# An encoder layer on one Trainium2 core: the 1024-token feed-forward block in two passes, its up-projection in seven block products

## The chip, the core and the metric

The kernel runs on one core of a Trainium2 chip. A core has five engines that run their own instruction queues in order and wait for one another by semaphores: PE (TensorE, matrix products), ACT (ScalarE), DVE (VectorE), POOL (GpSimd) and SP (SyncE, which issues nearly all of this kernel's DMAs). The metric is device time in microseconds (us) of one execution; lower is better.

## What is computed

One layer of an encoder with shared weights, on a request of 1024 tokens (the prompt) and one of 512 (the sample), width 1024, inner width 2816, all in float32:

```python
def encoder_layer(x, g_attn, w_in, ..., w_o, g_ffn, w_up, conv_w, conv_b, w_down):
    ...                                   # norm, attention in two branches, sigmoid gates: "merge"
    x = x + (g_a * a + g_b * bo) @ w_o
    u = dwconv(rmsnorm(x, g_ffn) @ w_up, conv_w, conv_b)      # w_up 1024 x 5632, conv of width 3 along the tokens
    u_gate, u_val = jnp.split(u, 2, axis=-1)
    return x + (jax.nn.gelu(u_gate) * u_val) @ w_down         # w_down 2816 x 1024

y = rmsnorm(encoder_layer(x, ...), g_final)
```

Only the last two lines of the layer and the final norm, and these for the prompt alone, are touched by the change: the feed-forward block, FFN from here on.

## The kernel before

Every float32 product is made of three matmuls on split operands: an operand is rounded to a `hi` part by ACT, and the rest, `lo = x - hi`, is made by DVE or POOL; then hi·hi, hi·lo and lo·hi are summed in PSUM (helper `mm3`, L147 to L149; for the down-projection L801 to L803 in `accumulate`). A matmul takes a 128x128 stationary block and streams 512 columns.

The sample runs first, then the prompt's attention, then `merge`, which leaves x as eight tiles `xacc` of 128 tokens x 1024, and then `ffn`. The order of each engine's instructions is fixed when the program is built; an engine never overtakes in its own queue.

`ffn` for the prompt (T = 1024, NT = 8 token tiles, FT = 22 channel blocks of 128):
- Norm, in two chunks of four token tiles: ACT sums the squares (L175) and takes the root (L176), DVE makes the reciprocal root in six small steps (L177 to L183) and `xn` (L190); PE transposes xn, eight times four 128x128 blocks a chunk (L198), ACT makes `hhi` from PSUM (L202) and DVE `hlo` (L203).
- For each of the 22 channel blocks: `wload` of 128 columns of w_up for the gate and for the value (a 512 KB DMA into `raw`, ACT makes `whi`, L138, DVE every third time and POOL otherwise make `wlo`, L141). `conv` sums 8 blocks of K over both halves of 512 tokens (L147 to L149), and ACT and DVE make the convolution (L831, L832, L834), GELU (L843) and the product (L848); ACT and POOL split it into `ghi`, `glo` (L851, L852).
- After every second channel block, `accumulate` multiplies the two blocks by their rows of w_down (L801 to L803) and DVE adds the sums to `xacc` (L805), so x stays in SBUF for the whole block and is updated eleven times.
- At the end the final norm, tile by tile (yo, L869), and a DMA for each tile.

The weights of the first channel blocks are loaded and split while `merge` still runs, since `raw`, `whi` and `wlo` come from pools that `merge` and `ffn` share.

Of the kernel before, what the change touches and what calls it, by code (L numbers as in the profile page):

```python
# [118 lines left out]
class _Layer:  # L119
# [687 lines left out]
    def ffn(self, ctx, hooks, xnp):  # L807
# [57 lines left out]
        for tt in range(NT):  # L865
# [3 lines left out]
            nc.vector.scalar_tensor_tensor(out=y, in0=x, scalar=rs, in1=gf, op0=ALU.mult, op1=ALU.mult)  # L869
            nc.sync.dma_start(self.y_dram[tt * P:(tt + 1) * P, :], y)  # L870

    def begin(self, ctx, x_dram, y_dram, T, side):
        self.x_dram, self.y_dram, self.side = x_dram, y_dram, side
        self.T, self.NT, self.NH, self.KPU = T, T // P, T // 512, 1024 // T
        self.stat_d = self.dram.tile([3, T, 8], F32, tag=f"stat{T}", name=f"stat{T}")
        self.frow_d = self.dram.tile([20, T], F32, tag=f"frow{T}", name=f"frow{T}")
        self.o_d = self.dram.tile([3, 2, P, T], F32, tag=f"o{T}", name=f"o{T}")
        self.ab_d = self.dram.tile([4, P, T], F32, tag=f"ab{T}", name=f"ab{T}")
        self.v_d = self.dram.tile([2, T, 512], F32, tag=f"v{T}", name=f"v{T}")
        self.hp = self.pool(ctx, "hp", 2 * KT // self.KPU)  # L880
# [17 lines left out]
def hybrid_encoder_kernel(ctx: ExitStack, tc: tile.TileContext, x_prompt, x_sample, g_attn, w_in, b_gate, rel_bias, sink,  # L898
# [63 lines left out]
    class _Taps:  # L962
        starts = (120, 164, 76)

        def __getitem__(self, key):
# [3 lines left out]

    w = {"w_in": w_in[0], "w_a_out": w_a_out[0], "w_b_out": w_b_out[0], "w_o": w_o[0], "w_up": w_up[0],  # L970
         "w_down": w_down[0]}
    raws = ctx.enter_context(tc.tile_pool(name="raw", bufs=3))
    split = ctx.enter_context(tc.tile_pool(name="split", bufs=3))

    class _W:
        def tile(self, *a, tag, **kw):
# [5 lines left out]
    with ExitStack() as s_ctx, ExitStack() as p_ctx:  # L982
        sample.begin(s_ctx, x_sample[0], y_sample[0], 512, left)
        with ExitStack() as a_ctx:
            sample.begin_norm(a_ctx, right)
            rp = a_ctx.enter_context(tc.tile_pool(name="rows", bufs=1, side=right, reuse_waits="tile"))
            sample.attention(a_ctx, bias_rows(rp))
        with ExitStack() as n_ctx:
            def begin_prompt():
                prompt.begin(p_ctx, x_prompt[0], y_prompt[0], 1024, right)  # L990
                prompt.begin_norm(n_ctx, right)
                return prompt.xin, "xin"
            sample.finish({11: lambda *a: prompt.norm_in(0, 4, *a), 15: lambda *a: prompt.norm_in(4, 4, *a)}, begin_prompt)
        s_ctx.close()
        with ExitStack() as a_ctx:
            prompt.attention(a_ctx, None)
        prompt.finish({})


# [24 lines left out]
```

## Time and profile before

| | us |
|---|---|
| median of three runs | 2368.64 (2364.14 to 2368.64) |
| the profiled execution | 2362.39, of it span 2360.6 |
| busy in the span: PE, DVE, ACT, POOL | 2273.1 (96%), 1110.5, 881.5, 563.6 |
| FFN of the prompt, first transposition to last matmul | 1592.2 to 2346.6 |
| from the last matmul to the end of the span | 14.0 |

All times below are from the start of the span. "Busy" of PE counts a matmul from its issue to its modelled end, and matmuls overlap: the mean duration of a matmul (395 ns) is not what it costs; the distance from one start to the next is. A group of rows shows what ended the idle time before its instructions, behind the arrow.

### The profile page before, as it was taken

To read this page: it belongs to the slowest core of one execution; us is meant where nothing else is said; L and a number is where in the kernel's file an instruction comes from. 1 tells how busy PE (TensorE), PEld (TensorE's weight loads), DVE (VectorE), ACT (ScalarE), POOL (GpSimd) and SP (SyncE) were. 2 spreads that over 40 slices of the span, in tenths; PEclk is the share of its full clock that TensorE was granted. 3 is DMA by queue.
4 is the path that set the end of the run, shared out by engine and by line. 5 is a ranking of instruction groups with operands and counts; after the bars stand their busy time and mean duration, and the time that the engine had idled before them with its cause. 6 is when DMAs were issued, how large, how long until landed. Compare 5 with 4: busy or idle time off the path is not lost.

```text
span 2360.6 us, 27878 instructions
## 1 busy us (share of the span) xinstructions
PE 2273.1 (96%) x10890; PEld 1864.3 (79%) x10890; DVE 1110.5 (47%) x1957; ACT 881.5 (37%) x1554; POOL 563.6 (24%) x296
## 2 busy tenths in 40 slices
PE   7999899899999999999999999999999999999997
PEld 6887687688878788898777788877888888888885
DVE  4547523644554535645784434335333433343336
ACT  5657422533443345655673111134212222212223
POOL 2121354333333210011002332231222212212220
PEclk9999999999999999999999999999999999999999
DMA  5553543333333312332118311112111111111101
GB/s 160 150 173 93 159 137 91 110 97 97 116 106 91 113 49 68 116 111 72 44 45 224 109 44 50 41 54 63 45 45 45 42 48 54 45 54 45 45 27 71
DMA packets 232856, 197.76 MB, mean 84 GB/s; under 512 B 18129, under 2 KB 203169, under 8 KB 232725
## 3 DMA queue, kind: packets, MB, share of 16 engines
q1 hardware_dynamic: 232440, 195.89, 27.6%
q8 instruction: 85, 1.39, 0.3%
q14 instruction: 47, 0.38, 0.1%
q10 hardware_dynamic: 284, 0.11, 0.0%
HBM read 175.19 MB, written 27.06 MB: 86 GB/s over the span
## 4 chain that ended last, share of the span: by engine, by line
PE 75%; DVE 3%; ACT 2%; issue 1%; POOL 0%; DMA 0%; POOLq 0%; ACTq 0%; DVEq 0%; SPq 0%
PE psu L147 10%; PE psu L149 10%; PE psu L148 10%; PE pacc L803 6%; PE pacc L802 6%; PE pacc L801 6%; PE psg L148 3%; PE psg L149 3%; PE psg L147 3%; PE pso L409 2%; PE pst L395 1%; PE psq L149 1%; PE psq L147 1%; PE psq L148 1%; PE psk L147 1%; PE psk L148 1%
## 5 line engine op out<-in xcount | busy, mean ns | idle before, releaser
L141 POOL TENSOR_TENSOR wlo<-raw,whi 128x1024 fp32r<-128x1024 f32 (+1 forms) x164 | 387.3, 2368 | 1170.3 <-ACT whi L138 946.3
L138 ACT CAST whi<-raw 128x1024 fp32r<-128x1024 f32 (+1 forms) x244 | 250.4, 1035 | 768.9 <-PE pacc L803 293.6
L805 DVE TENSOR_TENSOR xacc<-xacc,pacc 128x512 f32<-128x512 f32 x420 | 285.3, 686 | 303.2 <-PE pacc L803 301.0
L147 PE MATMUL psu<-hhi,whi 128*128 128x512 f32 x1056 | 416.5, 395 | 0.2 <-ACT hhi L202 0.2
L149 PE MATMUL psu<-hhi,wlo 128*128 128x512 f32 x1056 | 416.5, 395 | 0.0
L148 PE MATMUL psu<-hlo,whi 128*128 128x512 f32 x1056 | 416.3, 395 | 0.0
L141 DVE TENSOR_TENSOR wlo<-raw,whi 128x1024 fp32r<-128x1024 f32 (+1 forms) x80 | 103.8, 1298 | 328.2 <-ACT whi L138 305.6
L147 PEld LDWEIGHTS psu<-hhi,whi 128*128 128x128 f32 x1056 | 198.4, 188 | 46.5 <-ACT hhi L202 1.3
L149 PEld LDWEIGHTS psu<-hhi,wlo 128*128 128x128 f32 x1056 | 198.7, 188 | 45.8
L148 PEld LDWEIGHTS psu<-hlo,whi 128*128 128x128 f32 x1056 | 198.7, 188 | 45.6
L801 PE MATMUL pacc<-whi,ghi 128*128 128x512 f32 x528 | 209.5, 397 | 5.8 <-ACT ghi L851 4.2
L803 PE MATMUL pacc<-whi,glo 128*128 128x512 f32 x528 | 209.9, 398 | 2.3 <-POOL glo L852 2.3
L802 PE MATMUL pacc<-wlo,ghi 128*128 128x512 f32 x528 | 208.9, 396 | 0.0
L852 POOL TENSOR_TENSOR glo<-y,ghi 128x512 fp32r<-128x512 f32 (+1 forms) x44 | 81.1, 1842 | 451.4 <-ACT ghi L851 451.4
L832 DVE SCALAR_TENSOR_TENSOR y<-psu,vecs,y 128x511 f32<-128x511 f32 (+1 forms) x88 | 89.1, 1012 | 138.6 <-ACT y L831 138.6
L147 PE MATMUL psg<-hhi,whi 128*128 128x512 f32 x384 | 151.8, 395 | 1.2 <-ACT frow L505 1.2
L149 PE MATMUL psg<-hhi,wlo 128*128 128x512 f32 x384 | 151.7, 395 | 0.0
L148 PE MATMUL psg<-hlo,whi 128*128 128x512 f32 x384 | 151.6, 395 | 0.0
L801 PEld LDWEIGHTS pacc<-whi,ghi 128*128 128x128 f32 x528 | 99.6, 189 | 30.9 <-ACT ghi L851 5.1
L803 PEld LDWEIGHTS pacc<-whi,glo 128*128 128x128 f32 x528 | 99.5, 189 | 29.2 <-POOL glo L852 5.8
L802 PEld LDWEIGHTS pacc<-wlo,ghi 128*128 128x128 f32 x528 | 99.7, 189 | 23.4
L783 DVE TENSOR_TENSOR sg<-sg,psa 128x512 f32<-128x512 f32 x48 | 32.9, 687 | 157.1 <-PE psa L149 122.9
(150 smaller groups left out, 4156.1 us busy)
## 6 DMA issues: line engine op xcount, KB each, us to landing
raw<-in_w_up_dram SPq DMA_DIRECT2D x88, 512.0 KB
raw<-in_w_in_dram SPq DMA_DIRECT2D x80, 512.0 KB
raw<-in_w_down_dram SPq DMA_DIRECT2D x44, 512.0 KB
raw<-in_w_o_dram SPq DMA_DIRECT2D x16, 512.0 KB
skew<-rows SPq DMA_DIRECT2D x24, 256.0 KB
v<-vs SPq DMA_DIRECT2D x24, 256.0 KB
v<-v SPq DMA_DIRECT2D x24, 256.0 KB
out_dram<-yo SPq DMA_DIRECT2D x12, 512.0 KB
```

Of the source, the lines that this page charges most:

```text
L138: nc.scalar.copy(out=hi[:, :n], in_=raw[:, :n])
L141: eng.tensor_tensor(out=lo[:, :n], in0=raw[:, :n], in1=hi[:, :n].bitcast(F32), op=ALU.subtract)
L147: mm(out, whi, r[0], start=start, stop=False)
L148: mm(out, whi, r[1], start=False, stop=False)
L149: mm(out, wlo, r[0], start=False, stop=stop)
L409: mm(o[:, o0 * P:(o0 + n) * P], v[kt], p[:, c0 * P:(c0 + n) * P], start=i == 0, stop=i == total - 1)
L801: mm(p, a, whi[:, cols], start=i == 0, stop=False)
L802: mm(p, a, wlo[:, cols], start=False, stop=False)
L803: mm(p, b, whi[:, cols], start=False, stop=i == len(parts) - 1)
L805: nc.vector.tensor_tensor(out=x, in0=x, in1=p, op=ALU.add)
L832: nc.vector.scalar_tensor_tensor(out=y[:, 1:T], in0=ps[:, 0:T - 1], scalar=tap[0], in1=y[:, 1:T], op0=ALU.mult, op1=ALU.add)
L852: nc.gpsimd.tensor_tensor(out=lo, in0=yv, in1=hi.bitcast(F32), op=ALU.subtract)
```

## The change

The prompt's FFN is taken apart into three stages (`finish_strassen`); the sample's is as before.

`quads`: the same norm, but each chunk of four token tiles (a half of 512 tokens) is scaled by g and kept as float32 (`ht`, L905), x itself goes out to DRAM (`xres`, L897), and out of the four quadrants (two halves of K = 1024 by two halves of tokens) b11, b21, b12, b22 four combinations are made: t1 = b12 - b11, t3 = b22 - b12, t2 = b22 - t1, t4 = b21 - t2 (L915, three quarters on DVE and one quarter on POOL). The seven right operands b11, b21, t1, t2, t3, t4 and b22 are each split into hi and lo (L885, L886).

`up_strassen`: gate and value columns of a channel block are the two block rows of the left operand, and the two halves of K its block columns, so that a 2 x 2 by 2 x 2 block product gives gate and value for both halves of tokens. It is done by seven products of 12 matmuls (4 blocks of K, three each) in place of eight. POOL makes the four sums of weights (`rsum`, L968); `ring_split` makes hi (ACT, L938) and lo (DVE, L939) of each of the seven left operands in a ring of seven buffers, five products ahead. The products are summed in three PSUM banks A, B, C; ACT copies a bank out (L979, L983, L985, L988: `ug`, `uv`) and DVE adds B or C (L976). Convolution, GELU and product are as before, from SBUF in place of PSUM, and the result `gv` goes out to DRAM (L1004).

`down`: for each half of 512 tokens eight PSUM banks (4 token tiles by 2 halves of the width) sum over all 22 blocks (24 matmuls a step, L1056 to L1058); each step loads its 512 columns of `gv` (`graw`, L1036) and the 128 rows of w_down (`wraw`, L1038) into a ring of four buffers and splits them, three ring_splits a step. After the 22nd step DVE adds the eight sums to x, read back from DRAM (L1050), and the final norm of four tiles follows.

```diff
+    def quads(self, hc, psum, sm):
...
+        def split(name, src, pool, tag):
+            hi, lo = ([pool.tile([P, 2, H], F32R, tag=tag, name=f"{name}{s}") for _ in range(2)] for s in ("hi", "lo"))
+            for j in range(4):
+                h, l = hi[j // 2][:, j % 2], lo[j // 2][:, j % 2]
+                nc.scalar.copy(out=h, in_=src(j))
+                nc.vector.tensor_tensor(out=l, in0=src(j), in1=h.bitcast(F32), op=ALU.subtract)
...
+        for half in range(2):
...
+            for tt, (x, xn, rs) in enumerate(zip(xs, xns, self.rstd(xs, sm, lambda: next(left)))):
+                nc.vector.tensor_scalar(out=xn, in0=x, scalar1=rs, scalar2=None, op0=ALU.mult)
+                nc.sync.dma_start(self.x_d[half * 4 + tt], x)
...
+                    nc.tensor.transpose(ps[:, i * P:(i + 1) * P], xn[:, k * P:(k + 1) * P], self.c["ident"])
...
+                nc.scalar.activation(out=tiles[-1][:, k % 2], in_=ps, func=AF.Identity, scale=g[:, k:k + 1])
+                if half == 0 and k % 4 == 3:
+                    t = tiles[-2:]
+                    split(f"b{k // 4 + 1}1", lambda j: t[j // 2][:, j % 2], self.hp, "h")
...
+                eng = nc.gpsimd if j == 3 else nc.vector
+                eng.tensor_tensor(out=out[j], in0=in0[j], in1=in1[j], op=ALU.subtract)
+            split(name, lambda j: out[j], pool, tag)
+        combine("t1", b12, b11, b11, self.hp, "h")
+        t1 = b11
+        combine("t3", b22, b12, b12, hc, "hc")
+        split("b22", lambda j: b22[j], hc, "hc")
+        combine("t2", b22, t1, b22, self.hp, "h")
+        combine("t4", b21, b22, b21, hc, "hc")
...
+    def product(self, out, w, quad, start):
...
+        for j in range(4):
+            cols = slice(j * P, (j + 1) * P)
+            hi, lo = self.q[quad][j]
+            for n, (a, b) in enumerate(((whi, hi), (whi, lo), (wlo, hi))):
+                mm(out, a[:, cols], b, start=start and j == 0 and n == 0, stop=j == 3 and n == 2, skip_group_check=True)
...
+    def ring_split(self, src):
...
+        nc.scalar.copy(out=hi, in_=src)
+        nc.vector.tensor_tensor(out=lo, in0=src, in1=hi.bitcast(F32), op=ALU.subtract)
...
+    def up_strassen(self, ctx, psum):
...
+        for i in range(FT + 1):
+            cur = ["m1", "m2", "m5", "m6"] if i < FT else []
+            old = ["m4", "m3"] if i else []
+            order += [(i, m) for m in cur] + [(i - 1, m) for m in old] + ([(i, "m7")] if i < FT else [])
...
+                for out, a, b, op in ((s[0], blk("v", 0), blk("v", 1), ALU.add), (s[1], s[0], blk("g", 0), ALU.subtract),
+                                      (s[2], blk("g", 0), blk("v", 0), ALU.subtract), (s[3], blk("g", 1), s[1], ALU.subtract)):
+                    nc.gpsimd.tensor_tensor(out=out, in0=a, in1=b, op=op)
...
+            if m == "m1":
+                g["ug"], g["uv"] = (up.tile([P, T], F32, tag="uy", name=n) for n in ("ug", "uv"))
+                nc.scalar.copy(out=g["ug"][:, left], in_=g["A"])
...
+        where = {"m1": ("A", "b11"), "m2": ("B", "b21"), "m5": ("C", "t1"), "m6": ("A", "t2"), "m7": ("A", "t3"),
+                 "m4": ("A", "t4"), "m3": ("C", "b22")}
...
+    def down(self, ctx, psum):
...
+        def prepare(half, k):
+            graw = self.rraw.tile([P, 512], F32, tag="rraw", name="graw")
+            nc.sync.dma_start(graw, self.gv_d[k][:, half * 512:half * 512 + 512])
+            wraw = self.rraw.tile([P, D], F32, tag="rraw", name="wraw")
+            nc.sync.dma_start(wraw, W["w_down"][k * P:(k + 1) * P, :])
+            return self.ring_split(graw), [self.ring_split(wraw[:, nh * 512:nh * 512 + 512]) for nh in range(2)]
...
+                    mm(p, a, whi, start=k == 0, stop=False)
+                    mm(p, a, wlo, start=False, stop=False)
+                    mm(p, b, whi, start=False, stop=k == FT - 1)
...
+    def finish_strassen(self, w_ctx, h_ctx):
...
+                    w_ctx.close()
+                    self.rraw = self.pool(ring, "rraw", 4, side=other)
+                    self.rw = self.pool(ring, "rw", 7, side=other)
+                    self.rsum = self.pool(ring, "rsum", 6, side=other)
...
-    raws = ctx.enter_context(tc.tile_pool(name="raw", bufs=3))
-    split = ctx.enter_context(tc.tile_pool(name="split", bufs=3))
+    w_ctx = ctx.enter_context(ExitStack())
+    raws = w_ctx.enter_context(tc.tile_pool(name="raw", bufs=3, reuse_waits="tile"))
+    split = w_ctx.enter_context(tc.tile_pool(name="split", bufs=3, reuse_waits="tile"))
...
-        prompt.finish({})
+        prompt.finish_strassen(w_ctx, p_ctx)
```

The rows of the order that follow give line, operation, output and inputs, size, and how often it stands there in a row. Each engine's order up to the end of `merge` is as before, but for the splits of the first FFN weights, which stand among merge's last steps before and no longer do.

DVE, from the last addition of `merge` on. Before:

```order
L805 TENSOR_TENSOR xacc<-xacc,pacc 128x512 x2
L141 TENSOR_TENSOR wlo<-raw,whi 128x1024
L203 SCALAR_TENSOR_TENSOR hlo<-pst,vecs,hhi 128x512 x8
L177 RECIPROCAL rs<-rs 128x4
L179 TENSOR_SCALAR ms<-ms 128x4
L180 TENSOR_TENSOR ms<-ms,rs 128x4
L181 TENSOR_TENSOR ms<-ms,rs 128x4
L182 TENSOR_SCALAR ms<-ms 128x4
L183 TENSOR_TENSOR rs<-rs,ms 128x4
L190 TENSOR_SCALAR xn<-xacc,rs 128x1024 x4
L203 SCALAR_TENSOR_TENSOR hlo<-pst,vecs,hhi 128x512 x8
```

Now:

```order
L886 TENSOR_TENSOR b21lo<-ht,b21hi 128x512 x4
L177 RECIPROCAL rs<-rs 128x4
L179 TENSOR_SCALAR ms<-ms 128x4
L939 TENSOR_TENSOR rlo<-rraw,rhi 128x512
L180 TENSOR_TENSOR ms<-ms,rs 128x4
L939 TENSOR_TENSOR rlo<-rraw,rhi 128x512
L181 TENSOR_TENSOR ms<-ms,rs 128x4
L939 TENSOR_TENSOR rlo<-rsum,rhi 128x512
L182 TENSOR_SCALAR ms<-ms 128x4
L939 TENSOR_TENSOR rlo<-rsum,rhi 128x512
L183 TENSOR_TENSOR rs<-rs,ms 128x4
L939 TENSOR_TENSOR rlo<-rsum,rhi 128x512
```

The six small steps of the second half's norm and its four xn, which come right behind these rows, now stand behind eight splits of quadrants (four of b11, four of b21) and among five splits of weights.

POOL, over the same stretch. Before, from the last steps of `merge`:

```order
L786 TENSOR_TENSOR sg<-sg 128x512
L141 TENSOR_TENSOR wlo<-raw,whi 128x1024
L788 TENSOR_TENSOR mlo<-sg,mhi 128x512
L141 TENSOR_TENSOR wlo<-raw,whi 128x1024 x3
L852 TENSOR_TENSOR glo<-y,ghi 128x1024
```

Now:

```order
L786 TENSOR_TENSOR sg<-sg 128x512
L788 TENSOR_TENSOR mlo<-sg,mhi 128x512
L968 TENSOR_TENSOR rsum<-rraw 128x512
L968 TENSOR_TENSOR rsum<-rsum,rraw 128x512
L968 TENSOR_TENSOR rsum<-rraw 128x512
L968 TENSOR_TENSOR rsum<-rraw,rsum 128x512
L968 TENSOR_TENSOR rsum<-rraw 128x512
L968 TENSOR_TENSOR rsum<-rsum,rraw 128x512
L968 TENSOR_TENSOR rsum<-rraw 128x512
L968 TENSOR_TENSOR rsum<-rraw,rsum 128x512
L915 TENSOR_TENSOR ht<-ht 128x512
```

Eight sums of weights, all of whose inputs are loads, stand ahead of the first quarter that POOL subtracts for t1.

ACT, from the root of the second half's norm on. Before:

```order
L176 ACTIVATE rs<-ms,eps 128x4
L202 ACTIVATE hhi<-pst,vecs 128x512 x8
L138 CAST whi<-raw 128x1024
L831 ACTIVATE y<-psu,vecs 128x1024
L843 ACT_TABLE_LOAD
L843 ACTIVATE y<-y 128x1024
```

Now:

```order
L905 ACTIVATE ht<-pst,vecs 128x512 x8
L885 CAST t1hi<-ht 128x512 x4
L885 CAST t3hi<-ht 128x512 x4
L938 CAST rhi<-rsum 128x512
L885 CAST b22hi<-ht 128x512 x4
L938 CAST rhi<-rsum 128x512
L938 CAST rhi<-rraw 128x512
L885 CAST t2hi<-ht 128x512 x4
L938 CAST rhi<-rsum 128x512 x2
L885 CAST t4hi<-ht 128x512 x4
L979 COPY ug<-psuA 128x512
```

The first copy out of bank A, which the product m6 of the first channel block needs before it may write there, now stands behind the splits of all the combinations.

SP, at the end of the up-projection; before there was no such place, and its queue there only repeats this:

```order
L134 DMA raw<-in_w_up_dram 128x8x128 x2
L134 DMA raw<-in_w_down_dram 128x1024
L134 DMA raw<-in_w_up_dram 128x8x128 x2
L134 DMA raw<-in_w_down_dram 128x1024
L862 DMA gf<-in_g_final_dram 128x1024
```

Now:

```order
L1038 DMA wraw<-in_w_down_dram 128x1024
L1036 DMA graw<-gv 128x512
L1032 DMA gf<-in_g_final_dram 128x1024
L1050 DMA xres<-xres 128x1024 x4
L1038 DMA wraw<-in_w_down_dram 128x1024
L1036 DMA graw<-gv 128x512
L1050 DMA xres<-xres 128x1024 x3
L1004 DMA gv<-y 128x1024
L1038 DMA wraw<-in_w_down_dram 128x1024
L1036 DMA graw<-gv 128x512
```

The loads of x for both halves and of g_final now stand among the first steps' weights.

## Rows read from the trace of the kernel before

**Rows 1.** The page: busy time, granted PE clock in slices, chain that ended last

```profile
PE 2273.1 (96%) x10890; PEld 1864.3 (79%) x10890; DVE 1110.5 (47%) x1957; ACT 881.5 (37%) x1554; POOL 563.6 (24%) x296
...
PEclk9999999999999999999999999999999999999999
...
PE 75%; DVE 3%; ACT 2%; issue 1%; POOL 0%; DMA 0%; POOLq 0%; ACTq 0%; DVEq 0%; SPq 0%
```

**Rows 2.** Stretches: us, busy of PE, PEld, DVE, ACT, POOL, clock, DMA share, GB/s

```profile
1265.00:1295.00 30.00, 30.00 (x129) 23.91 (x127) 13.74 (x12) 8.98 (x11) 12.30 (x5) 1.00 0.98 252
1300.00:1310.00 10.00, 7.34 (x19) 4.92 (x20) 2.44 (x4) 2.25 (x4) 7.90 (x6) 0.69 0.92 302
1595.00:1600.00 5.00, 3.07 (x22) 2.66 (x22) 4.59 (x6) 2.76 (x5) 0.21 (x1) 1.00 0.72 208
1625.00:2325.00 700.00, 699.86 (x2994) 563.09 (x2992) 265.47 (x290) 153.96 (x145) 145.95 (x61) 1.00 0.15 44
```

**Rows 3.** PE's waits from 1592 us to the end: total, times, longest

```profile
PE pst L198 <- DVE hlo L203: 1.9, 1, 1.9
PE pacc L801 <- DVE xacc L805: 1.6, 2, 0.8
PE pacc L803 <- POOL glo L852: 1.3, 1, 1.3
PE psu L147 <- ACT hhi L202: 0.2, 1, 0.2
```

**Rows 4.** Timeline of PE at the start of the FFN: start, duration, instructions

```profile
1591.98 0.39 PE L803 MATMUL pacc<-whi,mlo 128*128 128x512 f32 x1
1592.21 1.91 PE L198 MATMUL pst<-ident,xn 128*128 128x128 f32 x16
1594.35 0.74 PE L147 MATMUL psu<-hhi,whi 128*128 128x512 f32 x2 [0.23 <-ACT hhi L202]
1597.01 0.66 PE L198 MATMUL pst<-ident,xn 128*128 128x128 f32 x4 [1.93 <-DVE hlo L203]
```

**Rows 5.** Groups by form, ACT: count, busy us, mean ns, idle before

```profile
L787 ACT CAST mhi<-sg 128x512 fp32r<-128x512 f32 x24 | 14.9, 621 | 84.0 <-POOL sg L786 84.0
L202 ACT ACTIVATE hhi<-pst,vecs 128x512 fp32r<-128x512 f32 x32 | 20.2, 687 | 7.1 <-PE pst L198 7.1
```

**Rows 6.** Groups by form, DVE and POOL, same columns

```profile
L399 DVE TENSOR_TENSOR ptlo<-pst,pthi 128x512 fp32r<-128x512 f32 x112 | 77.0, 688 | 14.2 <-ACT pthi L398 12.8
L834 DVE SCALAR_TENSOR_TENSOR y<-psu,vecs,y 128x1023 f32<-128x1023 f32 x44 | 56.4, 1281 | 1.1
L190 DVE TENSOR_SCALAR xn<-xacc,rs 128x1024 f32<-128x1024 f32 x12 | 8.7, 750 | 0.2
L183 DVE TENSOR_TENSOR rs<-rs,ms 128x4 f32<-128x4 f32 x4 | 2.8, 702 | 0.1
L181 DVE TENSOR_TENSOR ms<-ms,rs 128x4 f32<-128x4 f32 x4 | 0.6, 160 | 0.1
...
L788 POOL TENSOR_TENSOR mlo<-sg,mhi 128x512 fp32r<-128x512 f32 x24 | 31.6, 1320 | 12.1 <-ACT mhi L787 12.1
```

**Rows 7.** Timelines of POOL and DVE: the same subtraction beside POOL and alone

```profile
1592.84 2.38 POOL L141 TENSOR_TENSOR wlo<-raw,whi 128x1024 fp32r<-128x1024 f32 x1 [16.17 <-ACT whi L138]
...
1593.80 2.50 DVE L141 TENSOR_TENSOR wlo<-raw,whi 128x1024 fp32r<-128x1024 f32 x1 [0.70 <-ACT whi L138]
...
1627.32 1.21 DVE L141 TENSOR_TENSOR wlo<-raw,whi 128x1024 fp32r<-128x1024 f32 x1
```

**Rows 8.** Timeline of PE and its clock by microseconds, after waits late in the attention

```profile
1299.72 0.79 PE L148 MATMUL psa<-ablo,whi 128*128 128x512 f32 x1 [1.70 <-POOL ablo L718]
...
1301.00:1302.00 1.00, 1.00 (x3) 0.50 0.59 233
```

**Rows 9.** Timelines of PE and DVE at the end

```profile
2346.36 0.40 PE L803 MATMUL pacc<-whi,glo 128*128 128x512 f32 x1
...
2355.72 1.29 DVE L869 SCALAR_TENSOR_TENSOR yo<-xacc,rs,gf 128x1024 f32<-128x1024 f32 x1
```

More of the change, by code (lines that the diff above doesn't have):

```diff
@@ new lines, in product @@
+    def product(self, out, w, quad, start):
+        mm = self.nc.tensor.matmul
+        whi, wlo = w
+        for j in range(4):
+            cols = slice(j * P, (j + 1) * P)
[3 more added lines that the diff above has]
+    def ring_split(self, src):
+        nc = self.nc
+        hi = self.rw.tile([P, 512], F32R, tag="rhi", name="rhi")
+        lo = self.rw.tile([P, 512], F32R, tag="rlo", name="rlo")
+        nc.scalar.copy(out=hi, in_=src)
+        nc.vector.tensor_tensor(out=lo, in0=src, in1=hi.bitcast(F32), op=ALU.subtract)
+        return hi, lo
@@ new lines, in finish_strassen @@
+    def finish_strassen(self, w_ctx, h_ctx):
+        other = "left" if self.side == "right" else "right"
+        with ExitStack() as ring, ExitStack() as banks:
+            with ExitStack() as hctx:
+                with ExitStack() as outer:
+                    self.x = []
+                    self.xp = self.pool(outer, "xacc", self.NT)
+                    with ExitStack() as ctx:
+                        self.merge(ctx)
+                    w_ctx.close()
+                    self.rraw = self.pool(ring, "rraw", 4, side=other)
+                    self.rw = self.pool(ring, "rw", 7, side=other)
+                    self.rsum = self.pool(ring, "rsum", 6, side=other)
+                    hc = self.pool(hctx, "hc", 12, side=other)
+                    psum = self.pool(banks, "ups", 8, space=PSUM)
+                    sm = self.pool(outer, "fsm", 2)
+                    self.quads(hc, psum, sm)
+                with ExitStack() as ctx:
+                    self.up_strassen(ctx, psum)
+            h_ctx.close()
+            with ExitStack() as ctx:
+                self.down(ctx, psum)
```

116 lines of the change are left out of this document (added).

## The prediction

> **What bounds the kernel now.** I read the page first: PE is busy 96% of the span, the chain that ended last is PE for 75%, and PE's clock is near full in every slice [rows 1]. Then a long stretch of the block that is changed: in 700 us PE is busy for 699.86, issues 2994 matmuls at clock 1.00, and DVE, ACT and POOL are busy for 265, 154 and 146 us [rows 2]. So a matmul costs 700/2994 = 0.2338 us there, and nothing else has a price. The list of waits says the same: 5.0 us from 1592 us to the end [rows 3]. I call T the end of merge's last matmul, 1592.2 us [rows 4]; the FFN's last matmul ends at 2346.6 [rows 9], the span at 2360.6. Of the 754.4 us between, 44 x 2 x 8 x 3 = 2112 up matmuls and 22 x 8 x 2 x 3 = 1056 down matmuls take 3168 x 0.2338 = 740.7. The other 13.7 are 64 transpositions (16 in 1.91 us [rows 4]: 7.7), the 5.0 of waits, and 1.0 of rest.
>
> **The saved products.** Seven products of 12 matmuls for 22 channel blocks are 1848 matmuls in place of 2112: 264 x 0.2338 = **-61.7 us**, if PE still has no wait. The down-projection keeps its 1056, the norm its 64 transpositions. PE needs 84 x 0.2338 = 19.6 us for a channel block and 24 x 0.2338 = 5.6 us for a down step.
>
> **The up loop.** Per channel block ACT has 7 casts and 4 copies of 128x512 and three operations of 128x1024, at 0.62 for 512 columns [rows 5] and twice that for 1024: 10.6 us. DVE has 7 splits and 3 additions at 0.69, 4 taps at 1.28 [rows 6] and the product at 1.21 (the lone 128x1024 of [rows 7]): 13.2 us. POOL has 4 sums at 1.32 [rows 6]: 5.3 us. The loads (1.05 MB) and the write of gv (0.52 MB) are 80 GB/s, where [rows 2] show up to 302. All is below 19.6, and splits run five products ahead, some 14 us: 0.
>
> **DVE beside POOL.** One row of the trace changes the picture. DVE's subtraction of 128x1024 took 1.21 us alone, but 2.50 when it was issued at 1593.80 while POOL worked on its own from 1592.84 to 1595.22 [rows 7]: it ended about one lone duration after POOL's end. Four instructions on 128x4 (L183) have a mean of 0.70 us where a like one (L181) has 0.16 [rows 6]. So I take it that a DVE instruction that reads two tiles from SBUF waits until a running POOL instruction is through, and the other way round. In the up loop that costs nothing: even if DVE waits out all four sums, 13.2 + 5.3 = 18.5 is below 19.6. But the change also piles up such work where PE waits for it.
> The Trainium skill (SBUF — State Buffer, "Who interferes with whom") states that rule: an instruction of DVE with two SBUF inputs and one of GpSimd that reads SBUF take the same read interface in turn, and the second is blocked wholly. The row of 2.50 us agrees. By it this change comes to my forecast below; by durations of instructions that run alone, to the first rival.
>
> **The turn from merge to the first products.** Before, splits of the first weights were made during merge, and the first product ran 2.1 us after T [rows 4]. Now the new weight pools take the space of the old ones, so loads start about T and all preparation lies behind it, on ACT, DVE and POOL, with few products to cover it.
> First step, the second half's xn. ACT makes the last square (to T+2.1), 8 ht and 8 casts at 0.62 to 0.69 [rows 5] and the root: T+12.3. DVE, alone, ends four b21lo by T+12.9, then has six small steps of 0.17, five splits of 0.69 and the first xn of 0.75 [rows 6]: T+18.1. POOL's eight sums need the first four loads (2 MB behind the last writes of x; at 208 to 302 GB/s [rows 2] the first pair is there at about T+8). So from T+10.8, when the b21lo begin, six sums are still ahead, and DVE and POOL alternate: 6 x 1.32 = 7.9 us later, the first xn at T+26. Its transpositions, which follow the four xn and ACT's ht, take 5 us: **first product at T+31** (alone: T+23). PE had done the first half's transpositions at T+4.
> Second step, bank A. PE can run m1, m2, m5 of block 0, m1, m2 of block 1 and two matmuls: 62 x 0.2338 = 14.5 us, T+45.6, with 1.3 us for t1's lo on the way. Then m6 must write bank A, whose copy stands in ACT's queue behind 8 ht, 20 casts of combinations and 5 of weights: 33 x 0.63 = 20.8 us from T+28.5, and the copy 0.6. The casts also wait for POOL's four quarters of the combinations and a sum between them, 5 x 1.32 = 6.6: T+56.5. **PE waits about 11 us in all** (alone: 5.7; ACT then starts 8 us sooner and waits 1.3). Everything behind these rows has the same order on all engines and a lead that grows, so I add nothing more.
> So 31 + 11 = 42 us without a product before the loop runs, of which the 7.7 of transpositions are part.
> The clock: after 1.70 us of waiting PE's clock was at 0.50 a little later, the lower of its two levels, and three matmuls were issued in that microsecond [rows 8] where four or more fit at full speed. The turn has two idle stretches of over 10 us. In the first, the transpositions are paced by ACT and DVE, in the second the products behind it run slower: **+3 us** (bounds 0 and 6: the stretch from 1300 to 1310 at 0.69 has 10 x 0.31 = 3.1 us of it [rows 2], and there are two).
>
> **From up to down.** gf and eight tiles of x (4.7 MB with a gv between) stand in SP's queue ahead of the weights of the third and fourth steps, issued from about 8 us before the last up product, needed 17 and 22 us behind it. At 252 to 302 GB/s [rows 2] they are in after 16 to 19 us, at 208 after 23: 0 to 5, I take **+1**. The loop then loads 0.79 MB a step, 140 GB/s, 0.62 x 3 on ACT and 0.69 x 3 on DVE in 5.6 us: 0.
>
> **The end.** Before, 14.0 us: the last yo ended at 2357.0 and its DMA 3.6 later [rows 9]. Now eight additions keep pace with the last step's banks, four norms follow in place of the last five: 11.5 to 13.6, I take 13.5.
>
> **The sum.** From T to the span's end: 42 + 2904 x 0.2338 (679.0) + 3 + 1 + 13.5 = 738.5 against 768.4, with 1.0 of rest kept 739.5: **-29 to -30 us**, of the profiled 2362.4: 2333. The median of the runs shown is 6 above the profiled execution and their lowest 2; by the median it would be 2339. I take 2335.
>
> **The rivals.** (1) DVE and POOL don't hold each other up in the turn: first product at T+23 and 5.7 of waits, 13 us less: 2322, with a clean clock and a short end 2315. For it: the sums may come earlier or later than DVE's rows. Against: [rows 7]. Chance 0.25. (2) The turn costs more: all of POOL's twelve sums and quarters of that stretch come ahead of DVE's, and the clock takes its 6: 2350. Chance 0.15. (3) The down loop is starved, and the kernel becomes slower. A step needs 0.79 MB through a ring of four buffers, three times the rate of 44 GB/s of this block before [rows 2]; loads cannot run further ahead than two steps. The point: 30 us over 44 steps is 0.68 a step, a step of 6.3 us, 125 GB/s. At 100 GB/s a step takes 7.9 us, 44 x 2.3 = +101 on 2335: 2436. For it: each load waits for a split, which waits for a ring buffer. Against: 252 and 302 GB/s in [rows 2], with loads of the same size, and a lead of a step. Chance 0.06. (4) DVE becomes the bound of the up loop: from 19.6 + 30/22 = 21.0 us a block nothing is gained; at 22 it would be 2335 + 22 x 2.4 = 2388. Against: 18.5 with every sum waited out. Chance 0.04. That the change doesn't save the 264 matmuls is excluded by the order.
>
> **How the numbers follow.** Forecast 0.50, rivals 0.25, 0.15, 0.06, 0.04. Range 2314 to 2352: the forecast, (1), and (2) with the handover's upper bound. What a measurement can tell from no change is 0.2%, 4.7 us; faster 0.90, the same 0.03 (a starved loop or a DVE bound close to its point), slower 0.07.
>
> **What would show it.** PE: 84 matmuls per 19.6 us at clock 1.00 in the up loop, 24 per 5.6 in the down loop, no list entry of waits there over 2 us in total. In the turn: PE idle from about T+4 to T+26 for xn, then about 10 us for the copy of ug; DVE's splits there at 1.3 us and more where POOL runs, 0.69 where not. First product at T+23 would show the blocking wrong; long waits for wraw or graw in the down loop, or rlo as the releaser in the up loop, the forecast as a whole.

## The result and the profile after

The changed kernel takes 2315.99 us (median of 4 runs, 2312.19 to 2317.28) against 2368.64 (4 runs, 2364.14 to 2373.14): ratio 0.9775, 95% interval 0.9753 to 0.9797, 2.25% faster. The forecast was 2335 in a range of 2314 to 2352: the direction was right, the time lies near the low end, 19 us below the number. The execution profiled after took 2317.28 us, with a span of 2315.4.

The page of the kernel after, the lines that answer to [rows 1]:

```profile
PE 2207.3 (95%) x10626; PEld 1820.2 (79%) x10626; DVE 1238.4 (53%) x2143; ACT 1015.8 (44%) x1868; POOL 542.3 (23%) x322
...
PEclk9999999999999999999999899998899999999999
...
PE 78%; DVE 4%; ACT 2%; issue 2%; POOL 2%; DMA 1%; SPq 0%; DVEq 0%; ACTq 0%; POOLq 0%
```

There are 264 matmuls fewer, PE is still most of the chain, and its clock shows 8s in the two slices of the new turn (1563 to 1679 us), and one late in the attention, whose code is the same as before. The list of PE's waits of the kernel after, from 1585 us to the end, against [rows 3] (total, times, longest):

```profile
PE pst L902 <- DVE xn L896: 19.8, 1, 19.8
PE psuA L932 <- ACT ug L979: 6.5, 1, 6.5
```

Two waits, both in the turn; none in the up loop, at the handover or in the down loop. PE's timeline of the kernel after at the turn and at its last matmul (start, duration), against [rows 4, 9]:

```profile
1597.16 0.39 PE L803 MATMUL pacc<-whi,mlo 128*128 128x512 f32 x1
1597.39 3.65 PE L902 MATMUL pst<-ident,xn 128*128 128x128 f32 x32
1620.80 6.41 PE L902 MATMUL pst<-ident,xn 128*128 128x128 f32 x32 [19.75 <-DVE xn L896]
1626.96 0.48 PE L932 MATMUL psuA<-b11hi,rhi 128*128 128x512 f32 x1
...
1648.23 0.80 PE L932 MATMUL psuA<-t2hi,rhi 128*128 128x512 f32 x1 [6.51 <-ACT ug L979]
...
2303.44 0.39 PE L1058 MATMUL pacc<-rhi,rlo 128*128 128x512 f32 x1
```

T, the end of merge's last matmul, is 1597.4 here; it was 1592.2 before. Ahead of T the order is the same but for the first weights of the FFN; in the four experiments below that change nothing ahead of it T lies between 1594.1 and 1599.0, and the execution profiled before was 6 us faster than its kernel's median. Whether the change has a part in these 5 us is not shown; I leave them out. From T to the span's end it is 2315.4 - 1597.4 = 718.0 us, against 768.4 before and 738.5 forecast: **50.4 us less than before, 20.5 less than forecast.** The rest of this text accounts for both.

Stretches of the kernel after, columns as in [rows 2]; the last two lie in the up loop and in the down loop:

```profile
1610.00:1615.00 5.00, 0.00 (x0) 0.00 (x0) 5.00 (x6) 2.02 (x4) 4.92 (x4) 0.50 0.00 0
1615.00:1625.00 10.00, 4.21 (x19) 3.66 (x20) 9.91 (x16) 1.79 (x4) 3.72 (x3) 0.50 0.20 55
...
1650.00:1655.00 5.00, 5.00 (x16) 3.88 (x16) 5.00 (x6) 1.11 (x2) 4.28 (x3) 0.65 0.34 98
1655.00:1660.00 5.00, 5.00 (x23) 3.82 (x22) 2.84 (x5) 2.11 (x4) 0.35 (x1) 1.00 0.03 8
1700.00:1800.00 100.00, 100.00 (x434) 81.26 (x433) 69.76 (x76) 48.99 (x72) 29.69 (x21) 1.00 0.26 84
2100.00:2200.00 100.00, 100.00 (x443) 82.82 (x442) 45.66 (x90) 36.58 (x68) 0.00 (x0) 1.00 0.48 162
```

Both loops have PE busy for all of the time. Yet 434 and 443 matmuls stand in 100 us where [rows 2] had 2994 in 700, some 428 in 100: **the same matmul stands closer to the next one.** PE's timeline of the kernel after shows where; these are the first matmuls of successive products, each of 12:

```profile
1758.72 0.39 PE L932 MATMUL psuA<-t4hi,rhi 128*128 128x512 f32 x1
...
1761.48 0.39 PE L932 MATMUL psuC<-b22hi,rhi 128*128 128x512 f32 x1
...
1764.20 0.39 PE L932 MATMUL psuA<-t3hi,rhi 128*128 128x512 f32 x1
...
1766.92 0.40 PE L932 MATMUL psuA<-b11hi,rhi 128*128 128x512 f32 x1
...
1769.73 0.40 PE L932 MATMUL psuB<-b21hi,rhi 128*128 128x512 f32 x1
...
1780.93 0.39 PE L932 MATMUL psuC<-b22hi,rhi 128*128 128x512 f32 x1
```

The products of b22 and of t3 take 2.72 us each, 0.2267 a matmul; that of b11 takes 2.81, 0.2342 (b21, t1 and t2 are like it); t4 lies between with 2.76. From b22 to the next b22 it is 19.45 us for 84 matmuls, 0.2315 on average. In the down loop all are of the close kind: 54 matmuls from 2199.62 to 2211.86, 0.2267.

### The profile page after: what moved, and what is told of

It is laid out like the page before. It is cut to its first block, busy times and chain, and to the rows that moved or that the text cites. A ratio compares the mean times of both kernels' runs of the same rounds, so it can differ in the third digit from the quotient of the medians.

```text
span 2315.4 us, 28400 instructions
## 1 busy us (share of the span) xinstructions
PE 2207.3 (95%) x10626; PEld 1820.2 (79%) x10626; DVE 1238.4 (53%) x2143; ACT 1015.8 (44%) x1868; POOL 542.3 (23%) x322
## 4 chain that ended last, share of the span: by engine, by line
PE 78%; DVE 4%; ACT 2%; issue 2%; POOL 2%; DMA 1%; SPq 0%; DVEq 0%; ACTq 0%; POOLq 0%
PE psuA L932 10%; PE psuC L932 5%; PE pacc L803 4%; PE pacc L802 4%; PE pacc L801 4%; PE psg L147 3%; PE psg L149 3%; PE psg L148 3%; PE pacc L1058 3%; PE pacc L1056 3%; PE pacc L1057 3%; PE psu L147 3%; PE psu L149 3%; PE psu L148 3%; PE psuB L932 2%
## 5 line engine op out<-in xcount | busy, mean ns | idle before, releaser
L141 POOL TENSOR_TENSOR wlo<-raw,whi 128x1024 fp32r<-128x1024 f32 (+1 forms) x120 | 282.5, 2360 | 883.9 <-ACT whi L138 675.0
L805 DVE TENSOR_TENSOR xacc<-xacc,pacc 128x512 f32<-128x512 f32 x236 | 160.5, 688 | 144.7 <-PE pacc L803 142.7
L147 PE MATMUL psu<-hhi,whi 128*128 128x512 f32 x352 | 137.5, 391 | 0.0
L149 PE MATMUL psu<-hhi,wlo 128*128 128x512 f32 x352 | 137.4, 391 | 0.0
L148 PE MATMUL psu<-hlo,whi 128*128 128x512 f32 x352 | 137.1, 390 | 0.0
L1057 PE MATMUL pacc<-rlo,rhi 128*128 128x512 f32 x352 | 137.1, 389 | 0.0
L1058 PE MATMUL pacc<-rhi,rlo 128*128 128x512 f32 x352 | 137.0, 389 | 0.0
L1056 PE MATMUL pacc<-rhi 128*128 128x512 f32 x352 | 137.0, 389 | 0.0
L939 DVE TENSOR_TENSOR rlo<-wraw,rhi 128x512 fp32r<-128x512 f32 x88 | 57.3, 689 | 133.2 <-ACT rhi L938 133.2
L968 POOL TENSOR_TENSOR rsum<-rraw 128x512 f32<-128x512 f32 x44 | 65.7, 1493 | 267.2 <-DMA rraw<-in_w_up_dram 251.2
L938 ACT CAST rhi<-wraw 128x512 fp32r<-128x512 f32 x88 | 50.5, 618 | 147.3 <-PE pacc L1058 137.9
L938 ACT CAST rhi<-rsum 128x512 fp32r<-128x512 f32 x88 | 54.4, 622 | 117.7 <-PE psuC L932 71.2
L147 PE MATMUL psq<-hhi,whi 128*128 128x512 f32 x240 | 100.3, 418 | 1.1 <-DVE vb L341 0.6
L148 PE MATMUL psq<-hlo,whi 128*128 128x512 f32 x240 | 96.7, 403 | 0.0
```

Source lines behind the costliest of these rows:

```text
L141: eng.tensor_tensor(out=lo[:, :n], in0=raw[:, :n], in1=hi[:, :n].bitcast(F32), op=ALU.subtract)
L147: mm(out, whi, r[0], start=start, stop=False)
L148: mm(out, whi, r[1], start=False, stop=False)
L149: mm(out, wlo, r[0], start=False, stop=stop)
L805: nc.vector.tensor_tensor(out=x, in0=x, in1=p, op=ALU.add)
L938: nc.scalar.copy(out=hi, in_=src)
```

## Experiments

The theory when they began: the turn costs what the queues of DVE, ACT and POOL say, DVE and POOL hold each other up there, and the 20 us below the forecast come mostly from the matmul distance, which depends on where operands lie. Rivals stand with each run. Times of kernels are compared with runs of the kernel before on the same chip (2367 to 2369 us each time); for single times the distance from T to the span's end is the better measure, since T itself varies.

**POOL's sums of blocks 0 and 1 left out.** The weights themselves stand in for the sums in these two blocks, so their part of the output is not the reference's.

```diff
-                s = [self.rsum.tile([P, 512], F32, tag="rsum", name="rsum") for _ in range(4)]
+                s = [self.rsum.tile([P, 512], F32, tag="rsum", name="rsum") for _ in range(4)] if i > 1 else \
+                    [blk("v", 0), blk("g", 0), blk("v", 1), blk("g", 1)]
...
-                    nc.gpsimd.tensor_tensor(out=out, in0=a, in1=b, op=op)
+                    if i > 1:
+                        nc.gpsimd.tensor_tensor(out=out, in0=a, in1=b, op=op)
```

> The changed kernel with POOL's four sums of weights left out for the first two channel blocks (the raw blocks stand in for the sums there, so those two blocks' outputs are not the reference's). Theory 1 (a DVE instruction with two inputs in SBUF waits until POOL's is through): the four b21lo take 2.5 us in all where they took 5.72, the six small norm steps and five weight splits run at their lone durations, and PE's wait for the second half's xn falls from 19.8 us to 14 to 15; the wait for the copy of ug falls from 6.5 to some 4 to 6. Theory 2 (the xn are late because of ACT or the loads): 19.8 stays within 1 us.

2307.16 us (one time). DVE's and POOL's timelines of the kernel after, where the sums run:

```profile
1606.69 5.72 DVE L886 TENSOR_TENSOR b21lo<-ht,b21hi 128x512 fp32r<-128x512 f32 x4 [1.88 <-ACT b21hi L885]
...
1612.42 1.14 DVE L179 TENSOR_SCALAR ms<-ms 128x4 f32<-128x4 f32 x1
...
1618.90 3.74 DVE L896 TENSOR_SCALAR xn<-xacc,rs 128x1024 f32<-128x1024 f32 x4
...
1605.49 1.26 POOL L968 TENSOR_TENSOR rsum<-rraw 128x512 f32<-128x512 f32 x1 [26.23 <-DMA rraw<-in_w_up_dram]
...
1611.83 1.70 POOL L968 TENSOR_TENSOR rsum<-rraw 128x512 f32<-128x512 f32 x1
```

and DVE's and PE's of this kernel, without them:

```profile
1604.76 2.50 DVE L886 TENSOR_TENSOR b21lo<-ht,b21hi 128x512 fp32r<-128x512 f32 x4 [1.88 <-ACT b21hi L885]
...
1607.27 0.13 DVE L179 TENSOR_SCALAR ms<-ms 128x4 f32<-128x4 f32 x1
...
1610.62 2.73 DVE L896 TENSOR_SCALAR xn<-xacc,rs 128x1024 f32<-128x1024 f32 x4
...
1595.46 3.65 PE L902 MATMUL pst<-ident,xn 128*128 128x128 f32 x32
1611.50 6.36 PE L902 MATMUL pst<-ident,xn 128*128 128x128 f32 x32 [12.38 <-DVE xn L896]
1617.62 0.47 PE L932 MATMUL psuA<-b11hi,rhi 128*128 128x512 f32 x1
```

The same four subtractions take 5.72 us beside POOL and 2.50 alone, an instruction on 128x4 takes 1.14 or 0.13; the first product stands at T+22.2 in place of T+29.6, and T to the end is 709.9 in place of 718.0. The slow instruction on 128x4 ended at 1613.56, as POOL's sum of 1611.83 did (1613.53). DVE's splits also read the sums' results, but from 1606.69 to the last xn DVE has no idle time in this trace: its instructions last longer, it does not wait for data. So DVE and POOL do hold each other up, for 7.4 us of the turn, and POOL pays too: its sums are at 1.70 where the lone first one took 1.26. The wait for xn fell to 12.4 us, further than the 14 to 15 expected. Rival 1 of the prediction falls by this, although its time (2322 or 2315) is the one that came out: the right number would have come from a wrong reason.

**All combinations of the input on DVE**, none on POOL:

```diff
-                eng = nc.gpsimd if j == 3 else nc.vector
+                eng = nc.vector
```

> The changed kernel with all four quarters of each combination on DVE (POOL made one in four). Theory 1: POOL's 1.3 us a quarter and the DVE work that waits for it cost more than DVE's 0.65: PE's wait for the copy of ug falls from 6.5 us to 3 to 5, the wait for xn stays at 20, and the median comes to 2312 to 2316 against the changed kernel's 2316. Theory 2 (the quarters on POOL are hidden): wait 7 to 9, since DVE has more to do, median 2316 to 2319.

2315.01 us (2311.51 to 2317.03), ratio to before 0.9767 (0.9751 to 0.9784). The wait for ug falls from 6.5 to 4.0 us, that for xn stays (19.5). So the quarters' place is worth 2.5 us of that wait, with the time that DVE now spends on them already taken off; the prediction had put 6.6 us on these quarters and a sum together. From T to the end it is 714.4, 3.6 less, but the times of the two kernels overlap.

**Products earlier in the turn.** Both norms first; blocks 0 and 1 of m1, m2 and m5 are multiplied as soon as b11, b21 and t1 are there, with their preparation put between; t2 ahead of t3; ug copied early; combinations on DVE. The core of the edit:

```diff
+        first = [(0, "m1"), (1, "m1"), (0, "m2"), (1, "m2"), (0, "m5"), (1, "m5")]
+        order = [x for x in order if x not in first]
...
+        for x in first:
+            yield
+            prepare(*x)
+            multiply(*x)
+            if x in ((0, "m1"), (0, "m2")):
+                evacuate(*x)
```

> The changed kernel in another order of its turn: both halves' norm first, then the first half's transpositions, the splits of b11 and b21 with the products m1, m2 of blocks 0 and 1 between them, then the rest of the combinations (t2 ahead of t3), the first copy of ug straight after its product (in a buffer of its own), combinations wholly on DVE. Theory (PE stands still in the turn because DVE's xn stand behind splits that POOL holds up, and products that need only the first half are not used as cover): no single wait of 19.8 us; the first product some 8 to 12 us after merge in place of 29.6; but the sum of DVE's and POOL's work until the combinations are split stays, about 50 us, so many waits of 1 to 5 us take its place, 18 to 24 us in sum against 26.3: median 2308 to 2314. Rival (the turn is bound by the sum of ACT's, DVE's and POOL's work alone): sum of waits 26 or more, median 2316 or more.

2309.36 us (2308.69 to 2310.55), ratio 0.9746 (0.9729 to 0.9762): all four times lie below those of the changed kernel, though the intervals of the two ratios still overlap a little. PE's waits of this kernel, from 1585 us on:

```profile
PE psuA L940 <- ACT rhi L946: 6.5, 3, 4.3
PE psuB L940 <- ACT b21hi L885: 3.4, 1, 3.4
PE psuC L940 <- ACT t1hi L885: 2.4, 1, 2.4
PE psuC L940 <- DVE t1lo L886: 1.3, 1, 1.3
...
```

and one stretch of it, with columns as in [rows 2]:

```profile
1620.00:1625.00 5.00, 5.00 (x15) 4.00 (x14) 1.71 (x3) 0.52 (x2) 2.81 (x3) 0.50 0.27 81
```

The first product is at T+6.2, 23 us sooner and sooner than expected, and the waits sum to 15.5 us in place of 26.3 (18 to 24 was expected), but T to the end is only 6.3 us shorter (711.7). Of these, the combinations on DVE gave 3.6 by themselves in the experiment before; what each of the others is worth is not shown. The waits have moved to ACT's casts, mostly, and part of the early products ran at half the clock: 15 in these 5 us, where 23 fit at 1.00. I take it that the work of ACT and DVE ahead of the loop sets the turn's length, but no run shows that alone.

**Eight products instead of seven**, the two passes and the down-projection as in the changed kernel; the four quarters are split, nothing is combined or summed:

```diff
-        where = {"m1": ("A", "b11"), "m2": ("B", "b21"), "m5": ("C", "t1"), "m6": ("A", "t2"), "m7": ("A", "t3"),
-                 "m4": ("A", "t4"), "m3": ("C", "b22")}
...
-            bank, quad = where[m]
-            new = m in ("m1", "m2", "m5")
+            bank, quad = m[0] + m[2], f"b{int(m[1]) + 1}{'1' if m[2] == 'l' else '2'}"
+            new = m[1] == "0"
```

> The changed kernel without the Strassen step: two passes through DRAM and the same down stage, but the up-projection by eight products of four splits (b11, b21, b12, b22 all in the pool of high addresses, no combinations, no sums on POOL). Theory: 2112 matmuls for 1848, all at 0.234 us (place of the moving operand) = 494 us against 426; the turn is some 15 us shorter (no sums hold DVE up, 8 splits fewer on ACT and DVE, no wait for ug behind combinations), the down stage and the end stay 238 and 12. So 53 us more than the changed kernel: median 2362 to 2374, about the kernel before. Rival (the gain comes from the two passes and the down stage, not from the seven products): below 2345.

2367.19 us (2359.93 to 2369.79, 10 runs), ratio to before 0.9989 (0.9979 to 0.9999). Without the seven products nothing of the gain is left: here the passes through DRAM and the new down-projection cost what they give. PE's timeline of this kernel, the turn and two products, 11 apart, of the up loop:

```profile
1598.53 0.40 PE L803 MATMUL pacc<-whi,mlo 128*128 128x512 f32 x1
...
1607.67 7.34 PE L902 MATMUL pst<-ident,xn 128*128 128x128 f32 x47 [8.74 <-DVE xn L896]
...
1751.93 0.39 PE L923 MATMUL psuvr<-b22hi,rhi 128*128 128x512 f32 x1
...
1782.86 0.39 PE L923 MATMUL psugl<-b21hi,rhi 128*128 128x512 f32 x1
```

Here 132 matmuls take 30.93 us, 0.2343 each, and b22 is no faster than b21: it now lies in the pool of b21. From the end of merge to the span's end it is 766.9 us, 48.9 more than in the changed kernel. The sum: 264 matmuls at 0.2343 are 61.9, the closer distance of the seven is 1848 x (0.2343 - 0.2315) = 5.2, and its longer turn takes 15.4 back (first product at T+29.6 and 6.5 of waiting, against 8.7 + 12.0 here): 51.7 against the 48.9 measured. Of the 2.8 between, the slow clock behind the changed kernel's second wait (16 matmuls in 5 us where 23 follow) is 1.6 by estimate. One thing besides the products is different, though: in this program ACT takes the squares of the first half only after merge, in the changed kernel among merge's last additions, so that PE waits 8.7 us for the first xn. The frame by itself may thus gain up to 8.7 us on the kernel before (its down loop's closer matmuls, 1056 x 0.0060 = 6.3, and its end, 2.3 shorter, come to 8.6), and the seven products some 40 of the 48.9; no run has the eight products without that wait.

**The rows of w_down loaded twice**, to see how far the down loop is from starving:

```diff
             nc.sync.dma_start(wraw, W["w_down"][k * P:(k + 1) * P, :])
+            nc.sync.dma_start(wraw, W["w_down"][k * P:(k + 1) * P, :])
```

> The changed kernel with each load of w_down's rows issued twice in the down stage, so that a step moves 1.31 MB in place of 0.79 in 5.4 us (240 GB/s). Theory (the down loop is far from starved): PE waits for a load for less than 10 us in sum over the 44 steps, the time rises by 0 to 10 us. Rival (it was close to the point where the loads bound it): each step takes 6 us and more, 25 to 90 us more.

2321.68 us (one time); T to the end 720.9. The stretch in its down loop that answers to the last one above:

```profile
2100.00:2200.00 100.00, 100.00 (x443) 82.84 (x442) 45.74 (x90) 36.43 (x69) 0.00 (x0) 1.00 0.74 256
```

At 256 GB/s in place of 162 PE is as busy as before; waits of 1.6 us are added, in the loop's last 110 us. Rival 3 was far off.

**Where the operands lie.** What sets 0.2267 or 0.234 is the question of the seven experiments that follow. First t1 and t3 exchange pools (their place in the loop stays), then the kernel before with the two sides of SBUF exchanged, then the changed kernel with them exchanged:

```diff
-        combine("t1", b12, b11, b11, self.hp, "h")
+        combine("t1", b12, b11, b11, hc, "hc")
...
-        combine("t3", b22, b12, b12, hc, "hc")
+        combine("t3", b22, b12, b12, self.hp, "h")
```

> The changed kernel with t1 and t3 exchanged in their places: t1's parts lie in the pool where t3's lay, and the other way round. In the trace of the changed kernel a matmul of the up loop follows the one before at 0.2266 us for the products with b22 and t3 (whose parts lie at the low addresses of SBUF) and at 0.231 to 0.238 for those with b11, b21, t1, t2 (high addresses). Theory 1 (where the moving operand lies sets the distance between matmuls): t1's products (m5) now run at 0.2266 and t3's (m7) at 0.231 to 0.238. Theory 2 (the place in the loop sets it): m5 stays slow and m7 fast. The time is the same within 2 us either way.

```diff
-    left = nc.default_side
-    right = "right" if left == "left" else "left"
+    right = nc.default_side
+    left = "right" if right == "left" else "left"
```

> The kernel before with the two sides of SBUF exchanged: the prompt's pools at the low addresses, the sample's at the high ones; nothing else. Theory (the place of the moving operand sets the distance between matmuls): the prompt's 3744 matmuls that stream its normed input (2112 of the up-projection, 1632 of the projections) go from 0.234 to 0.227 us, the sample's 1872 the other way: 1872 x 0.0073 = 14 us less, median 2350 to 2358 against 2368; in the prompt's FFN the up matmuls follow at 0.227. Rival (place matters only in the changed kernel's loops): same time within 4 us, 0.234 as before.

> The changed kernel with the two sides of SBUF exchanged: b11, b21, t1, t2 now lie at 17 to 79 KB of a partition, b22, t3, t4 at 119 to 165, the ring of split weights (stationary in the up loop, both operands in the down loop) at 179 to 207. Theory (the place of the moving operand alone counts, high is slow): m1, m2, m5, m6 at 0.227 us, the down stage slow at 0.234 (from 0.2257). Rival (moving and stationary operand must lie on the same side to be fast): m1, m2, m5, m6 stay at 0.234 since their weights are now at the other end, and the down stage stays at 0.226 since both its operands lie together.

With the pools of t1 and t3 exchanged the distances are exchanged too: PE's timeline of that kernel has t3 now at 2.80 us a product and t1 at 2.74 (the time 2313.03, once).

```profile
1760.26 0.40 PE L932 MATMUL psuA<-t3hi,rhi 128*128 128x512 f32 x1
...
1763.06 0.40 PE L932 MATMUL psuA<-b11hi,rhi 128*128 128x512 f32 x1
...
1768.68 0.40 PE L932 MATMUL psuC<-t1hi,rhi 128*128 128x512 f32 x1
...
1771.42 0.40 PE L932 MATMUL psuA<-t2hi,rhi 128*128 128x512 f32 x1
```

So it is the place. The kernel before with its sides exchanged takes 2352.16 us (2345.25 to 2356.37), ratio 0.992 (0.9894 to 0.9946): some 17 us from a change that does no work. One stretch of its FFN, and the same stretch of the kernel before:

```profile
1700.00:1900.00 200.00, 200.00 (x877) 164.34 (x876) 79.01 (x87) 44.57 (x42) 43.08 (x18) 1.00 0.17 49
```

```profile
1700.00:1900.00 200.00, 200.00 (x857) 161.12 (x856) 76.58 (x84) 43.47 (x41) 42.39 (x18) 1.00 0.16 48
```

877 matmuls against 857. In the changed kernel the exchange gave 2326.27 (once; T at 1608.4, T to the end 716.1) and left each product as it was (b22 2.72 us, b11 2.81), although b11 now lies low and b22 high: the height does not matter. The next two move the ring of split weights next to b11's pool, alone and with the early products:

```diff
-                    self.rw = self.pool(ring, "rw", 7, side=other)
                     self.rsum = self.pool(ring, "rsum", 6, side=other)
-                    hc = self.pool(hctx, "hc", 12, side=other)
+                    hc = self.pool(ring, "hc", 12, side=other)
+                    self.rw = self.pool(ring, "rw", 7, side=other)
```

> The changed kernel with the ring of split weights moved up, next to the pool of b11, b21, t1, t2: it now lies at 93 to 125 KB of a partition in place of 33 to 61, b22, t3, t4 just below it at 45 to 91. Theory (a matmul follows the one before at 0.2266 us where moving and stationary operand lie within some 80 KB of each other, and at 0.231 to 0.238 from some 105 KB on): t2 (163 to 177) and most of t1 (179 to 193) become fast, b21 and b11 (195 to 221) partly, b22, t3, t4 stay fast: 264 x 0.0075 = 2 us for each product that turns, 4 to 8 us in all, median 2308 to 2312. Rival (the boundary is a fixed address between 121 and 159 KB, on either side of which both must lie): no product of the four turns, t4 stays, median 2314 to 2318.

> The order of the third experiment and the placing of the ninth together. Theory: both gains add, 6 and 4 to 8 us: median 2301 to 2306. Rival of the ninth: 2308 to 2311.

2316.46 us (2312.83 to 2321.95) and 2315.94 (2310.49 to 2317.55): no product changed, so it is not how far the operands lie apart. The moved ring also changed the order of the turn. In the first kernel the first product came at T+20.6 in place of T+29.6, yet T to the end stayed at 718.8, once more a sooner start without a gain. The second missed its 2301 to 2306: its waits sum to 20.9 us instead of 15.5, with the first product at T+13.3 instead of T+6.2. The last two shift everything on the left by 32 bytes:

```diff
+    nc.gpsimd.memset(const.tile([P, 8], F32, name="pad"), 0.0)
     c["eps"] = const.tile([P, 1], F32, name="eps")
```

> One 32-byte tile is added to the constants, so that every buffer on the left side of SBUF moves by 32 bytes and the right side stays; the program is otherwise the changed kernel. Counted from the buffers' places in it: in the changed kernel 3360 of the 7944 matmuls of 512 columns have a moving operand whose address differs from that of the stationary one by 32 bytes modulo 64, with the pad none (before: 4416 of 8208; before with its sides exchanged 2016). Theory ALIGN (the distance of 0.234 us is the price of that difference): the products of b11, b21, t1 and t2 fall from 0.2338-0.2346 to 0.2267 us like those of b22 and t3, and so do the prompt's projections and its merge ahead of T. Up loop 1056 x 0.0075 = 8 us less (T to the span's end 718 to 710 us), ahead of T 2304 x 0.007 = 16 us less; in all 2316 to 2292 us (2287 to 2298). Rival SIDE (what counts is the side of SBUF itself, whatever the address): no product changes, 2312 to 2320 us.

> The kernel with both norms first, the early copy of ug, blocks 0 and 1 of m1, m2 and m5 early and all combinations on DVE (2309.4 us) with the same 32-byte pad; 3360 differing matmuls become none here too. ALIGN: 2309 to 2285 us (2280 to 2291), first product still about T+6, all products of 512 columns at 0.2267 us except t4. SIDE: 2306 to 2312 us. A third outcome, that the gains do not add (as with the moved ring, which undid the early products), would show 2292 us as with the pad alone and a turn as long as there.

2315.07 us (2311.88 to 2317.03) and 2306.74 (2299.31 to 2311.51). PE's timeline of the first:

```profile
1760.24 0.39 PE L932 MATMUL psuC<-b22hi,rhi 128*128 128x512 f32 x1
...
1762.96 0.39 PE L932 MATMUL psuA<-t3hi,rhi 128*128 128x512 f32 x1
...
1765.68 0.40 PE L932 MATMUL psuA<-b11hi,rhi 128*128 128x512 f32 x1
...
1768.47 0.40 PE L932 MATMUL psuB<-b21hi,rhi 128*128 128x512 f32 x1
```

b11 takes 2.79 us in place of 2.81, b22 and t3 2.72 as ever: equal remainders modulo 64 bytes are not the cause, and 24 us that I expected did not come. The second, with the early products, is the fastest kernel of the study (ratio 0.9738, 0.9719 to 0.9758), but its interval overlaps that without the pad, so nothing is claimed for the pad.

**What stays open.** "Both operands from the same side" holds for every product of the FFN's up-projection, but not for the down-projection before, where both lie on one side and 22 matmuls took 1733.00 - 1727.88 = 5.12 us, 0.2327 (PE's timeline of the kernel before):

```profile
1727.88 0.39 PE L801 MATMUL pacc<-whi,ghi 128*128 128x512 f32 x1
...
1733.00 0.39 PE L802 MATMUL pacc<-wlo,ghi 128*128 128x512 f32 x1
```

Counted from the buffers' places in the compiled programs, one rule fits the matmuls of 512 columns of these kernels: the close distance goes with equal remainders of the two operands' addresses modulo 512 bytes. In the changed kernel the difference is 0 for b22, t3, t4 and the new down-projection and 416 for b11, b21, t1 and t2 (384 with the pad); in the kernel before it is 128 for the old down-projection. Of the FFN's products only t4, with its 2.76 us, is between the two. It has not been tried, and it is a fit, not a cause shown. The trial would be a pad of 416 bytes in place of 32. If the fit holds, an estimate from the rows above is 3360 matmuls of the changed kernel x 0.0075 = 25 us.

## Why the prediction was right, and where it was off

**The saved products** carried the forecast and were right: 84 matmuls a block, no wait of PE in either loop, DVE 70 us busy of 100 in the up loop, and eight products in the same frame give the gain away. Rivals 3 and 4 never came near.

**The mis-sized term is the 0.2338 us per matmul** in "2904 x 0.2338", taken from a stretch before and kept for code whose operands lie elsewhere. From the first product (1626.96) to the end of the last matmul (2303.67) it is 676.7 us; without the 6.5 of the second wait 670.2, against 679.0 + 3 for the clock. The up products were at 0.2315 (1848 x 0.0023 = 4.2 us less), those of the down loop at 0.2267 (1056 x 0.0071 = 7.5 less): 11.7 us of the 11.8. That leaves 3 for the clock, as it was put, but as a remainder: it was not measured by itself. The step that failed is the silent one, that a matmul of one shape at full clock has one price; [rows 2] mixed the up- and down-projection and showed a mean only.

**The turn** had the right releasers in the right order, xn by DVE and then the copy of ug, at T+23.4 and T+50.8. The first product came at T+29.6 where T+31 was said, by two errors that partly cancel: xn was there 2.6 us sooner (T+26 was said), but the transpositions behind it took 6.2 us, at a clock of 0.50, where 5 was put. The second wait was 6.5 and not "about 11": PE was ready at T+44.3 (T+45.6 was said), and the copy was done at T+50.8, 5.7 us sooner than said. ACT's timeline of the kernel after:

```profile
1623.21 5.01 ACT L905 ACTIVATE ht<-pst,vecs 128x512 f32<-128x512 f32 x8 [11.18 <-PE pst L902]
...
1638.79 1.23 ACT L885 CAST t2hi<-ht 128x512 fp32r<-128x512 f32 x2 [2.73 <-DVE ht L915]
1642.34 1.14 ACT L885 CAST t2hi<-ht 128x512 fp32r<-128x512 f32 x2 [2.32 <-POOL ht L915]
...
1647.61 0.57 ACT L979 COPY ug<-psuA 128x512 f32<-128x512 f32 x1
```

ACT began at T+25.8 where T+28.5 was said, its 33 operations took 18.4 us and not 20.8, and it waited 6.0 us where 6.6 was put; but only 2.3 of these were for POOL, 3.7 were for DVE, which the prediction had not named there. Together the turn was 6 us shorter than said, so rival 2 did not come either.

**DVE beside POOL** was right, and reached further than "an instruction that reads two tiles": the row of 1.14 us is a TENSOR_SCALAR with one input. The Trainium skill (SBUF — State Buffer, "Who interferes with whom") says that a tensor_scalar can enter a mode that takes both ports and then contends with GpSimd as well; the pair 1.14 and 0.13 agrees.

**Handover and end.** The handover cost 0 where 1 was put, and the end 11.7 (2303.67 to 2315.4) where 13.5 was taken out of 11.5 to 13.6; the kernel with eight products has the same end, so it belongs to the new down-projection. The sum of the account: 29.6 + 6.5 + 670.2 + 11.7 = 718.0; off by 1.4 + 4.5 + 11.8 + 1 + 1.8 = 20.5 us. All errors behind T had one sign, which is why a range that was built from the turn's bounds held the time only at its edge. That it held it is luck in part: its lower end, 2314, goes back to rival 1, whose mechanism the first experiment refutes.

## What to carry to other kernels

Price a matmul from rows with the same operands in the same places, not from the mean of a stretch: two pairs of buffers of one shape differed by 3% here, and a mere exchange of sides was worth 0.8% of the kernel. Where a loop is bound by PE, fewer products pay in full, and what is lost is lost in the turn ahead of it: sum up the queues of the engines that prepare it, and keep GpSimd out of a stretch in which DVE is the one waited for. A run with the old count of products in the new frame tells what the idea itself is worth, if the rest of the order stays, which here it did not quite.

## What the runs showed of the hardware

With PE's clock at 1.00 and no wait, matmuls of 128x512 (fp32r) stand 0.2267 us apart or, as the mean of a product, 0.230 to 0.235, by where their two operands lie in SBUF, not by height, distance or remainder modulo 64 bytes. The Trainium skill (SBUF — State Buffer, "Who interferes with whom") gives PE two read ports that are independent of each other, by which I would expect the place not to matter. The rows show that it does, for a reason that is left open here. And GpSimd pays for the conflict as DVE does: its sums of 128x512 took 1.26 us alone and 1.70 beside DVE.
